# Opening of a hybrid decoder block: first two token tiles transposed before the norm's factor is known, the factor multiplied in later

## The chip, the cores and the metric

The kernel runs on one core of a Trainium2 chip. The core has a matrix engine (TensorE, PE in the profile, with its weight loads as PEld), three engines for elementwise work (VectorE as DVE, ScalarE as ACT, GpSimd as POOL) and SyncE (SP), which here only issues DMA transfers. Every engine works through its own queue in order and waits on semaphores for the others. PE writes to PSUM, eight banks of 128 partitions by 512 fp32 columns; GpSimd works on SBUF alone in this kernel. The metric is device time in microseconds (us).

## What is computed

A decoder block on 512 tokens of width 1024 in fp32: a conformer convolution branch and a gated linear recurrence branch, merged by sigmoid gates, then a SwiGLU mixer and a last norm. The change touches only the first two lines of it:

```python
def rmsnorm(x, g):
    xf = x.astype(jnp.float32)
    y = xf * lax.rsqrt(jnp.mean(xf * xf, axis=-1, keepdims=True) + EPS)
    return (y * g.astype(jnp.float32)).astype(x.dtype)
...
        h = rmsnorm(x, norm1_g[l])
        z = h @ w_in[l] + b_in[l]
        z_glu, z_rx, z_rg, z_ga, z_gb = jnp.split(z, split_idx, axis=-1)
        u = z_glu[..., :D_CONV] * jax.nn.sigmoid(z_glu[..., D_CONV:])
...
        m = jax.nn.sigmoid(z_ga) * y_a + jax.nn.sigmoid(z_gb) * y_b
        x = x + m @ w_mix_out[l]
        h = rmsnorm(x, norm2_g[l])
        x = x + (jax.nn.silu(h @ ffn_w1[l]) * (h @ ffn_w3[l])) @ ffn_w2[l]
    return rmsnorm(x, norm_f_g)
```

The norm's factor belongs to a token: the square root of the mean square of its row of x. The gain g belongs to a channel.

## The kernel before

The 512 tokens are four tiles of 128 (`xt[t][h]`, tile t, half h of the 1024 channels). The products need h with channels on partitions, so x is transposed on PE, 128 by 128 at a time, into PSUM. Eight blocks of channels (c = 0 to 7) make up the 1024. From each transposed block ACT makes a rounded high part and DVE the low part that is left (`h1p[c]`, in the profile h10h, h10l to h17h, h17l); weights are split alike into `hl_in`, high part first. A product is then three matmuls for each block, high by high, low by high, high by low weights (`mm3`, line 525).

The opening (lines 639 to 665) is written out by hand for PE, ACT, DVE and SP: what stands there is the order of these queues. The order of GpSimd and of everything after line 665 is made by a scheduler. PE first runs 21 warm-up matmuls that feed nothing (line 504). `norm1_rows` squares and sums the two halves of a tile on ACT, takes the root there, inverts it on DVE, and DVE multiplies both halves of x by it (line 595). When tiles 0 and 1 are scaled, `turn_half` (line 567) transposes them into banks and splits them (ACT line 582, DVE line 583). These are the first half of the columns, tokens 0 to 255. `early_mm` then multiplies them with the weight chunks in0 and in8, the first two of the order in line 233, into the first half of the banks z0 and z8, and the low products of each come last. Meanwhile tiles 2 and 3 are normed; they are transposed and split, and `early_mm` fills the second halves. z1, the product with chunk in1, is the first on all 512 tokens (`in_mm`, line 675). DVE casts and subtracts in8 itself there, through `Later`; GpSimd subtracts in0.

SP issues the four halves of x0 and x1 first, then a row of gains, then the chunks in0 and in8, 512 KB each, then x2 and x3. Six PSUM banks rotate under the tag "mm", two under "cv"; four raw weight buffers and five split ones rotate too. At most eight transfers are under way, since the ninth waits for the first one's semaphore.

## Time and profile before

| what | us |
|---|---|
| median of 3 runs (lowest, highest) | 797.65 (797.45, 798.82) |
| profiled execution, own time | 797.7 |
| its span, first to last instruction | 795.9 |
| PE busy in the span | 789.2 |
| DVE, ACT, POOL busy | 673.2, 471.7, 228.8 |

The span is what the trace covers; the execution's own time has 1.8 us more around it. In the rows that follow, a timeline row gives start, duration, engine, line of the kernel, operation, what is written from what, shapes and count, and in brackets the idle time of that engine before the row with what ended it. Matmuls overlap, so that the start of one to the start of the next, not the printed duration, is what one costs. A row of a group gives busy time in all and the mean ns of one, then the idle time before them.

### The profile page before, as it was taken

How to read it: one execution, taken by the hardware profiler on the slowest of the kernel's cores; microseconds unless marked ns; L12 is line 12 of the kernel's file. 1: busy time of each engine (PE TensorE's matmuls, PEld its weight loads, DVE VectorE, ACT ScalarE, POOL GpSimd, SP SyncE). 2: the span in 40 equal slices, each digit the busy share in tenths (PEclk: the TensorE clock that was granted, in tenths of full speed). 3: DMA queues.
4: the chain of work that ended last, by engine and by line, in shares of the span. 5: the costliest groups of instructions: out<-in, count | busy, mean ns of one | idle time of the engine just before them, and what ended most of it. 6: DMA issues, size and time to landing. Idle time of an engine off the chain costs nothing.

```text
span 795.9 us, 12177 instructions
## 1 busy us (share of the span) xinstructions
PE 789.2 (99%) x4369; PEld 690.5 (87%) x4369; DVE 673.2 (85%) x1020; ACT 471.7 (59%) x683; POOL 228.8 (29%) x181
## 2 busy tenths in 40 slices
PE   9999999999999999999999999999999999999997
PEld 8888888888888888888888898999999999888885
DVE  6699899999989988786787889978878887889757
ACT  6646585987768855563335575545455555577443
POOL 1855766797666856030000000000000000000000
PEclk9999999999999999999999999999999999999999
DMA  6945646487555664368847545566555553676652
GB/s 213 257 130 143 187 144 208 121 247 208 173 168 173 213 182 120 128 203 263 276 160 243 172 134 158 131 171 181 155 133 133 133 133 106 210 258 207 198 173 106
DMA packets 184604, 140.29 MB, mean 176 GB/s; under 512 B 14259, under 2 KB 162143, under 8 KB 184543
## 3 DMA queue, kind: packets, MB, share of 16 engines
q1 hardware_dynamic: 183103, 134.27, 55.2%
q0 software_dynamic: 1440, 5.24, 3.5%
q8 instruction: 34, 0.56, 0.3%
q14 instruction: 27, 0.22, 0.1%
HBM read 113.79 MB, written 18.64 MB: 166 GB/s over the span
## 4 chain that ended last, share of the span: by engine, by line
PE 99%; DVE 0%; issue 0%; ACT 0%
PE z L534 36%; PE or L953 13%; PE ft L1080 7%; PE yb L534 7%; PE fa L1080 7%; PE fr L1080 6%; PE ya L534 5%; PE mxr L953 5%; PE fe L1080 4%; PE g L827 3%; PE fb L1080 2%; PE f L534 2%; PE warm L506 1%; PE f L1106 1%; PE tx L574 1%; PE th L574 0%
## 5 line engine op out<-in xcount | busy, mean ns | idle before, releaser
L702 DVE SCALAR_TENSOR_TENSOR cv<-u,par,cv 128x511 f32<-128x511 f32 (+19 forms) x240 | 162.4, 730 | 5.0 <-ACT cv L699 4.7
L119 POOL TENSOR_TENSOR hl_in<-raw_in,hl_in 128x1024 fp32r<-128x1024 f32 x51 | 123.5, 2426 | 83.1 <-ACT hl_in L123 69.6
L355 POOL DMA_DIRECT2D raw_fb<-raw_fb x10 | 8.7, 874 | 298.4 <-DVE raw_fb L357 186.1
L119 POOL TENSOR_TENSOR ows<-ows 128x256 f32<-128x256 f32 x66 | 56.7, 861 | 37.7 <-DMA ows<-in_ffn_w_dram 34.7
L123 ACT CAST hl_ft<-raw_fb 128x1024 fp32r<-128x1024 f32 x40 | 41.8, 1048 | 32.5 <-DVE raw_fb L357 17.0
L123 ACT CAST hl_in<-raw_in 128x1024 fp32r<-128x1024 f32 x50 | 52.1, 1043 | 10.4 <-PE z L534 6.6
L119 DVE TENSOR_TENSOR hl_ft<-raw_fb,hl_ft 128x1024 fp32r<-128x1024 f32 x40 | 48.5, 1220 | 7.0 <-ACT hl_ft L123 6.9
L119 DVE TENSOR_TENSOR hl_fb<-raw_fb,hl_fb 128x1024 fp32r<-128x1024 f32 x30 | 36.6, 1221 | 9.5 <-ACT hl_fb L123 9.3
L357 DVE TENSOR_TENSOR raw_fb<-raw_fb,raw_fb 128x1024 f32<-128x1024 f32 x20 | 24.5, 1225 | 20.3 <-DMA raw_fb<-in_ffn_w_dram 20.0
L534 PE MATMUL z<-h10h,hl_in 128*128 128x512 f32 (+1 forms) x108 | 41.5, 385 | 0.0
L534 PE MATMUL z<-h17h,hl_in 128*128 128x512 f32 (+1 forms) x108 | 41.1, 381 | 0.0
L534 PE MATMUL z<-h13h,hl_in 128*128 128x512 f32 (+1 forms) x108 | 41.1, 381 | 0.0
L534 PE MATMUL z<-h15h,hl_in 128*128 128x512 f32 (+1 forms) x108 | 41.1, 381 | 0.0
L534 PE MATMUL z<-h14h,hl_in 128*128 128x512 f32 (+1 forms) x108 | 41.1, 381 | 0.0
L534 PE MATMUL z<-h16h,hl_in 128*128 128x512 f32 (+1 forms) x108 | 41.1, 381 | 0.0
L534 PE MATMUL z<-h12h,hl_in 128*128 128x512 f32 (+1 forms) x108 | 41.1, 381 | 0.0
L534 PE MATMUL z<-h11h,hl_in 128*128 128x512 f32 (+1 forms) x108 | 41.1, 381 | 0.0
L123 ACT CAST hl_fb<-raw_fb 128x1024 fp32r<-128x1024 f32 x30 | 31.4, 1047 | 8.9 <-PE mxr L953 3.7
L119 DVE TENSOR_TENSOR hl_ob<-raw_ob,hl_ob 128x1024 fp32r<-128x1024 f32 (+1 forms) x23 | 27.0, 1174 | 11.0 <-ACT hl_ob L123 10.9
L123 ACT CAST hl_ob<-raw_ob 128x1024 fp32r<-128x1024 f32 (+1 forms) x23 | 23.3, 1015 | 21.6 <-PE or L953 10.8
L1080 PE MATMUL fe<-hs_0h,hl_ft 128*128 128x256 f32 x160 | 30.7, 283 | 0.0
L1080 PE MATMUL ft<-hs_1h,hl_ft 128*128 128x256 f32 x160 | 30.4, 283 | 0.0
(1016 smaller groups left out, 2610.0 us busy)
## 6 DMA issues: line engine op xcount, KB each, us to landing
raw_in<-in_w_in_dram SPq DMA_DIRECT2D x52, 512.0 KB
raw_fb<-in_ffn_w_dram SPq DMA_DIRECT2D x96, 256.0 KB
ows<-in_ffn_w_dram SPq DMA_DIRECT2D x44, 256.0 KB
os<-ows SPq DMA_DIRECT2D x22, 512.0 KB
raw_ob<-in_ffn_w_dram SPq DMA_DIRECT2D x33, 256.0 KB
raw_ot<-os SPq DMA_DIRECT2D x33, 256.0 KB
raw_lo<-in_lru_w_out_dram SPq DMA_DIRECT2D x16, 320.0 KB
raw_fb<-raw_fb POOLq DMA_DIRECT2D x10, 512.0 KB, 4.6
```

The source lines that it names most:

```text
L119: return eng.tensor_tensor(out=o, in0=x, in1=y, op=ALU.subtract)
L123: copy(h, full)
L355: pool_e.dma_start(out=q, in_=y, accum_op=ALU.add)
L357: vec.tensor_tensor(out=q, in0=q, in1=y, op=ALU.add)
L506: pe.matmul(wp[:, :P], ones, ones, start=True, stop=True)
L534: pe.matmul(ps, l, r, start=i == 0, stop=i == n - 1)
L574: pe.transpose(ps[:, t * P : (t + 1) * P], src, ident)
L702: vec.scalar_tensor_tensor(out=acc[c][:, s:], in0=u[c][:, : T - s], scalar=dw(c, s), in1=acc[c][:, s:], op0=ALU.mult, op1=ALU.add)
L827: pe.matmul(ps, l, r, start=k == 0, stop=k == len(mms) - 1)
L953: pe.matmul(banks[i], l_[:, ts], r_, start=start and n == 0, stop=stop and n == 2, skip_group_check=again)
L1080: pe.matmul(ps[:, HALVES[i]], lw[:, 4 * i + c, :], rx_, start=not (again or i or c or m), stop=bool(i and c == 3 and m == 2), skip_group_c ...
L1106: pe.matmul(plain_1[:, cs], l, r, start=k == 0 and m == 0, stop=k == ND - 1 and m == 2)
```

## The change

The first two tiles are transposed as they land, half a tile at a time, and unscaled: `load_x` issues single halves, in0's chunk is loaded and cast in two halves (`FirstChunk`), and the first half of z0's product starts when the first four blocks of channels of x0 and x1 are there. Two `plain` sets of split tiles hold the unscaled blocks. The warm-up is 6 matmuls ahead and 1 between. The norm's factor of a token is laid on the diagonal of a 128 by 128 tile (`dg`) and multiplied by ones, which puts it on all partitions with tokens along columns (`rp`, copied to `rbc`). It multiplies the first halves of z0 and z8 in place (`scale_early`), and the kept transposes of tiles 0 and 1, whose scaled blocks (`scaled`) are split into the first halves of `h1p` for z1 and all later products. GpSimd is now in the order written by hand, casts in8 and in1 besides, and makes four of the eight low parts of tiles 0 and 1.

```diff
-WARM = 21
+WARM = 6, 1
...
+    PAIRED = (0, 4, 1, 5, 2, 6, 3, 7)
...
+    def place(banks, c):
+        return banks[c % 4][:, HALVES[c // 4]]
+    def turn_rows(banks, t, cs):
+        for c in cs:
+            pe.transpose(place(banks, c)[:, (t % 2) * P : (t % 2 + 1) * P], xt[t][c // 4][:, (c % 4) * P : (c % 4 + 1) * P], ident)
+    def split_rows(banks, hf, cs):
+        for c in cs:
+            ps = place(banks, c)
+            g = pc("norm1_g", c)
+            h, l = parts_in(hf)[c]
+            act.activation(h, ps, AF.Copy, scale=g)
+            vec.scalar_tensor_tensor(out=l, in0=ps, scalar=g, in1=h.bitcast(F32), op0=ALU.mult, op1=ALU.subtract)
...
+        def cast(self, h):
+            cs = slice(h * T, (h + 1) * T)
+            vec.tensor_copy(self.hl[:, 0, cs], self.raw[:, cs])
+            sub(pool_e, self.hl[:, 1, cs], self.raw[:, cs], self.hl[:, 0, cs].bitcast(F32))
...
-    with tc.manual_schedule(engines={ET.PE, ET.Activation, ET.DVE, ET.SP}):
-        norm1_rows(0)
-        norm1_rows(1)
+    with tc.manual_schedule(engines={ET.PE, ET.Activation, ET.DVE, ET.SP, ET.Pool}):
+        w0 = FirstChunk()
+        load_x(0, [0])
+        load_rows(first[0])
+        load_x(1, [0])
+        w0.load(0)
+        load_x(0, [1])
+        load_x(1, [1])
+        w0.load(1)
+        warm_up(WARM[0])
         rows_turned(0, ROWS[0][1])
...
+        turn_rows(banks0, 0, range(4))
+        turn_rows(banks0, 1, range(4))
+        warm_up(WARM[1])
+        w0.cast(0)
+        split_rows(banks0, 0, range(4))
...
+        early_mm(0, 0, range(4), (0, 1))
+        turn_rows(banks0, 0, range(4, 8))
+        turn_rows(banks0, 1, range(4, 8))
+        early_mm(0, 0, range(4), (2,))
...
+        split_rows(banks0, 0, range(4, 6))
+        dg = shortt("dg")
+        for t in range(2):
+            vec.tensor_scalar(out=dg[:, t * P : (t + 1) * P], in0=ident, scalar1=r[t], scalar2=None, op0=ALU.mult)
+        split_rows(banks0, 0, range(6, 8))
+        early_mm(0, 0, range(4, 8), (0, 1))
...
+        emit_to(2, pool_e.tensor_copy)
+        early_mm(0, 0, range(4, 8), (2,))
+        rp = bank2("rp")
+        for t in range(2):
+            pe.matmul(rp[:, t * P : (t + 1) * P], ones, dg[:, t * P : (t + 1) * P], start=True, stop=True)
...
+        def scale_early(i):
+            ps = early[i][2][:, HALVES[0]]
+            vec.tensor_tensor(out=ps, in0=ps, in1=rbc, op=ALU.mult)
+        def scaled(c):
+            f = scaled1[c // 2][:, HALVES[c % 2]]
+            vec.scalar_tensor_tensor(out=f, in0=place(banks0, c), scalar=pc("norm1_g", c), in1=rbc, op0=ALU.mult, op1=ALU.mult)
...
+        for c in (2, 6, 3, 7):
+            scaled(c)
+        for c in (2, 6, 3, 7):
+            scaled_parts(c, vec)
...
-        mm3(ps, ws, h1)
+        mm3(ps, [ws[k] for k in PAIRED], [h1[k] for k in PAIRED])
```

Three places of the queues. First ACT, from its first square of x (n1j00 is tile 0, half 0; tx00 to tx07 are the banks of the transposes) on; before:

```order
L550 ACTIVATE n1j00_185,stats_162<-x00_114 128x512
L556 ACTIVATE n1j01_186,stats_162<-x01_115 128x512
L557 ACTIVATE stats_162<-stats_162 128x1
L550 ACTIVATE n1j10_194,stats_162<-x10_116 128x512
L556 ACTIVATE n1j11_195,stats_162<-x11_117 128x512
L557 ACTIVATE stats_162<-stats_162 128x1
L582 ACTIVATE h10h_163<-tx00_211,par_108 128x256
L582 ACTIVATE h11h_165<-tx01_216,par_108 128x256
```

and with the change (hp0h to hp3h hold the high parts of the unscaled blocks, two blocks each; tx00 to tx03 are banks of two blocks):

```order
L559 ACTIVATE n1j00_193,stats_136<-x00_114 128x512
L627 ACTIVATE hp0h_153<-tx00_189,par_108 128x256
L627 ACTIVATE hp0h_153<-tx01_190,par_108 128x256
L627 ACTIVATE hp1h_155<-tx02_191,par_108 128x256
L627 ACTIVATE hp1h_155<-tx03_192,par_108 128x256
L565 ACTIVATE n1j01_194,stats_136<-x01_115 128x512
L566 ACTIVATE stats_136<-stats_136 128x1
L559 ACTIVATE n1j10_195,stats_136<-x10_116 128x512
L565 ACTIVATE n1j11_196,stats_136<-x11_117 128x512
L566 ACTIVATE stats_136<-stats_136 128x1
L627 ACTIVATE hp2h_157<-tx00_189,par_108 128x256
L627 ACTIVATE hp2h_157<-tx01_190,par_108 128x256
```

Four copies moved ahead of three of the squares; the other four stay behind them.

Second SP, its first transfers; before:

```order
L490 DMA x00_114<-in_x_dram 128x512
L490 DMA x01_115<-in_x_dram 128x512
L490 DMA x10_116<-in_x_dram 128x512
L490 DMA x11_117<-in_x_dram 128x512
L483 DMA rows0_109<-in_norm1_g_dram 8x128
L167 DMA raw_in0_206<-in_w_in_dram 128x8x128
L167 DMA raw_in8_251<-in_w_in_dram 128x8x128
L490 DMA x20_118<-in_x_dram 128x512
```

and with the change:

```order
L500 DMA x00_114<-in_x_dram 128x512
L493 DMA rows0_109<-in_norm1_g_dram 8x128
L500 DMA x10_116<-in_x_dram 128x512
L660 DMA raw_in0_171<-in_w_in_dram 128x4x128
L500 DMA x01_115<-in_x_dram 128x512
L500 DMA x11_117<-in_x_dram 128x512
L660 DMA raw_in0_171<-in_w_in_dram 128x4x128
L150 DMA raw_in8_268<-in_w_in_dram 128x8x128
L500 DMA x20_118<-in_x_dram 128x512
```

The first half of x1 moved up from third to second of the large transfers, half of the weights to third; the second halves of x0 and x1 moved down.

Third POOL, from its first subtraction of weights; before, these were

```order
L119 TENSOR_TENSOR hl_in0_208<-raw_in0_206,hl_in0_208 128x1024
L119 TENSOR_TENSOR hl_in1_384<-raw_in1_382,hl_in1_384 128x1024
L119 TENSOR_TENSOR hl_in9_439<-raw_in9_437,hl_in9_439 128x1024
L119 TENSOR_TENSOR hl_in16_478<-raw_in16_476,hl_in16_478 128x1024
L119 TENSOR_TENSOR hl_in17_483<-raw_in17_481,hl_in17_483 128x1024
```

and with the change (hq0 and hq2 hold scaled blocks):

```order
L119 TENSOR_TENSOR hl_in0_172<-raw_in0_171,hl_in0_172 128x512 x2
L123 CAST hl_in8_292<-raw_in8_268 128x1024
L119 TENSOR_TENSOR hl_in8_292<-raw_in8_268,hl_in8_292 128x1024
L119 TENSOR_TENSOR h10l_138<-hq0_161,h10h_137 128x256
L119 TENSOR_TENSOR h14l_146<-hq2_163,h14h_145 128x256
L123 CAST hl_in1_377<-raw_in1_274 128x1024
L119 TENSOR_TENSOR hl_in1_377<-raw_in1_274,hl_in1_377 128x1024
L119 TENSOR_TENSOR h11l_140<-hq0_161,h11h_139 128x256
L119 TENSOR_TENSOR h15l_148<-hq2_163,h15h_147 128x256
L119 TENSOR_TENSOR hl_in9_424<-raw_in9_280,hl_in9_424 128x1024
```

Two casts, one whole subtraction (in8) and four quarter ones are new there.

More of the change, by code (lines that the diff above doesn't have):

```diff
@@ L161, in emit_chunk @@
         rv = raw[:, :n]
-        if where == "made":
+        if where in ("made", "there"):
             pass
@@ L504, in tile_block, with warm_up @@
     wp = bank2("warm")
-    for _ in range(WARM):
-        pe.matmul(wp[:, :P], ones, ones, start=True, stop=True)
+    def warm_up(n):
+        for _ in range(n):
+            pe.matmul(wp[:, :P], ones, ones, start=True, stop=True)
     first = [i for i, (lo, _, _) in enumerate(parts) if lo < n_first]
-    load_x(0)
-    load_x(1)
-    load_rows(first[0])
     def rows_turned(c0, c1):
@@ new lines, in tile_block, with early_mm, row_junk @@
+    todo_in = {}
+    def early_mm(i, hf, ks, parts):
+        _, ws, ps = early[i]
+        for k in ks:
+            (wh, wl), (xh, xl) = ws[k], parts_in(hf)[k]
+            for n in parts:
+                l, r = ((wh, xh), (wh, xl), (wl, xh))[n]
+                left = todo_in.setdefault((i, hf), 3 * ND)
+                todo_in[i, hf] = left - 1
+                pe.matmul(ps[:, HALVES[hf]], l, r, start=left == 3 * ND, stop=left == 1)
+    def row_junk(t):
+        return [shortt(f"n1j{t}{h}") for h in range(2)]
@@ new lines, in tile_block @@
+        scaled(4)
+        scaled_parts(0)
+        scaled_parts(4)
+        scaled(1)
+        scaled(5)
+        scale_early(0)
+        scale_early(1)
+        banks1 = [b(f"tx1{i}") for i, b in enumerate((bank2, bank2, bank, bank))]
+        turn_rows(banks1, 2, PAIRED)
+        turn_rows(banks1, 3, PAIRED)
+        emit_to(3, pool_e.tensor_copy)
+        split_rows(banks1, 1, range(8))
+        scaled_parts(1)
+        scaled_parts(5)
+        for k in range(4):
+            for i in range(2):
+                early_mm(i, 1, [k], (0, 1))
```

98 lines of the change are left out of this document (69 added, 29 removed).

## The prediction

> **What bounds the kernel now.** I read the page's busy times first, then the chain of waits in order of time.
>
> ```profile
> span 795.9 us, 12177 instructions
> PE 789.2 (99%) x4369; PEld 690.5 (87%) x4369; DVE 673.2 (85%) x1020; ACT 471.7 (59%) x683; POOL 228.8 (29%) x181
> ```
>
> ```profile
> 1.09 7.80 PE warm L506 x42
> 8.89 0.15 PE par_ps L517
> 9.04 1.90 PE tx L574 x16
> 10.94 6.51 PE z L534 x48
> 17.45 2.13 PE tx L574 x16
> 19.58 2.87 PE z L534 x24
> 22.44 0.07 PE par_ps L517
> 22.52 2.92 PE z L534 x24
> 25.43 0.29 PE par_ps L517 x3
> 25.72 43.59 PE z L534 x192
> ...
> 685.94 104.37 PE or L953 x458
> ```
>
> The reader is to see that TensorE (PE) never rests between 1.09 and 790 us, so that the time is the sum of its matmuls plus a start of 1.1 and a tail of 5.6 us. The only part of that sum that makes nothing is the 7.80 us of warm-up. It stands for the time until both tiles of the first half are loaded, normed and scaled. All the change can do is to begin the real work earlier than 8.89, and it must hand that lead on to the first full-width product, z1, which begins at 25.72 in the chain.
>
> The next view splits the warm-up at 7.08 (start:end, length, PE busy and passes).
>
> ```profile
> 1.08:7.08 6.00, 5.99 (x28) 1.00 0.82 258
> 7.08:8.83 1.75, 1.75 (x16) 1.00 1.18 315
> ```
>
> 28 passes in 6.00 us are 0.214 each, 16 in 1.75 are 0.109: the matrix clock doubles at about 7.1 us, though the column of the granted clock (1.00) does not show it. Work brought forward into the first 7 us thus runs at half speed.
>
> **The change part by part.** *Removed and added on PE.* 21 warm-up matmuls of two passes become 7: 28 passes fewer, of which 16 at 0.109 and 12 at 0.214 are 4.3 us. Added are the two matmuls that spread the norm's factor over all partitions (rp): 4 passes, 0.45 us. The 32 transposes and 96 half-width products stay. At most 3.9 us can be won, and only if what feeds PE keeps up. So I follow the feeders.
>
> ```profile
> 3.41 0.63 ACT L550 ACTIVATE n1j<-x 128x512 f32<-128x512 f32 x1 [0.99 <-DMA x<-in_x_dram]
> 4.41 0.63 ACT L556 ACTIVATE n1j<-x 128x512 f32<-128x512 f32 x1 [0.27 <-DMA x<-in_x_dram]
> 5.81 0.63 ACT L550 ACTIVATE n1j<-x 128x512 f32<-128x512 f32 x1 [0.36 <-DMA x<-in_x_dram]
> 6.54 0.63 ACT L556 ACTIVATE n1j<-x 128x512 f32<-128x512 f32 x1
> 7.30 0.30 ACT L557 ACTIVATE stats<-stats 128x1 f32<-128x1 f32 x1
> 9.45 0.47 ACT L582 ACTIVATE h10h<-tx,par 128x256 fp32r<-128x256 f32 x1 [1.85 <-PE tx L574]
> 9.82 0.47 ACT L582 ACTIVATE h11h<-tx,par 128x256 fp32r<-128x256 f32 x1
> 9.16 0.68 DVE L123 CAST hl_in<-raw_in 128x1024 fp32r<-128x1024 f32 x1
> 9.96 0.48 DVE L583 SCALAR_TENSOR_TENSOR h10l<-tx,par,h10h 128x256 fp32r<-128x256 f32 x1
> 10.36 0.48 DVE L583 SCALAR_TENSOR_TENSOR h11l<-tx,par,h11h 128x256 fp32r<-128x256 f32 x1
> ```
>
> *Landings.* ScalarE (ACT) waited for the first, second and third transfer of 256 KB until 3.41, 4.41 and 5.81; the fourth kept nobody past 6.54. The SyncE queue now brings x0 first half, x1 first half, first half of in0's weights, x0 and x1 second halves, second half of the weights, all 256 KB. I give these slots 3.4, 4.4, 5.8, 6.6, 7.4 and 8.4 (the last two one slot of about 0.9 further each).
>
> *First half of z0.* 12 warm passes of 0.214 end at 3.7; the transpose of the gains and four of x0 at half speed take PE to 4.8, four of x1 to 5.6, the single warm-up matmul to 6.0. ACT's first copy of a transposed bank can start some 0.4 after its last transpose (9.45 against the second transpose in the old order), so at 5.3, then every 0.36 (9.82 - 9.45): free at 6.75. VectorE (DVE) casts half of the weights (half of 0.68) once they are there, 5.8 to 6.15, and then makes four low parts, one every 0.39 (10.36 - 9.96), to 7.7. PE's eight products run between 6.1 and 7.9. The first product starts 4.6 us earlier than the old 10.7. That lead does not last.
>
> *Second half of z0.* PE does eight transposes and four low products, to about 9.4. But ACT, free at 6.75, has three squares and two roots ahead of the next copies: a square takes 0.73 (6.54 - 5.81), a root 0.2 to 0.3, so 3 x 0.73 + 0.5 puts the fifth copy at 9.4, its end at 9.9. DVE's low parts follow at 0.39 with two multiplications for the diagonal between them. Such a multiplication is priced from the first row below, a quarter of 0.483, so 0.13 with rounding up: the eighth low part is ready at 9.9 + 3 x 0.39 + 0.26 + 0.48 = 11.8. PE, which stands still for some 1.5 us in here, ends z0's half at 12.0, four low products at 12.5, rp at 13.0.
>
> ```profile
> L595 DVE TENSOR_SCALAR x<-x,stats 128x512 f32<-128x512 f32 x8 | 3.5, 483 | 0.1
> L558 DVE RECIPROCAL stats<-stats 128x1 f32<-128x1 f32 x4 | 0.6, 162 | 2.5 <-ACT stats L557 2.5
> L119 POOL TENSOR_TENSOR hl_in<-raw_in,hl_in 128x1024 fp32r<-128x1024 f32 x10 | 23.9, 2401 | 25.8 <-ACT hl_in L123 14.3 <-DVE hl_in L123 8.6 <-issue 2.9
> L119 POOL TENSOR_TENSOR hl_gate<-raw_gate,hl_gate 128x512 fp32r<-128x512 f32 x1 | 1.3, 1284 | 2.0 <-ACT hl_gate L123 2.0
> L215 POOL MEMSET raw_gate<- 128x512 f32 x2 | 1.1, 528 | 0.1
> ```
>
> *in8's weights go to GpSimd (POOL).* Its cast of 1024 columns is not in this trace. Below it lies the fill (0.53 for 512 columns, so 1.06), above it the two-input subtraction, 2.40. DVE casts the second half of in0's weights at 8.6 (behind its statistics), so POOL ends their subtraction (1.28) at 10.2, so the cast is done at 11.3 to 12.6, before PE wants it at 13.0, and the low part at 13.7 to 15.0, wanted at 13.0 + 16 x 0.12 = 14.9. I take the middle, 1.7: hidden, with 1.1 us to spare for the high and 0.6 for the low part; beyond that it costs PE one for one. [...]
>
> *From z8 on.* The marks are z8's first product, the transposes, the second half, z1.
>
> ```profile
> 14.40 0.28 PE L534 MATMUL z<-h10h,hl_in 128*128 128x256 f32 x1
> ...
> 17.28 2.30 PE L574 MATMUL tx<-ident,x 128*128 128x128 f32 x16
> 19.33 0.36 PE L534 MATMUL z<-h10h,hl_in 128*128 128x256 f32 x1
> ...
> 25.52 0.47 PE L534 MATMUL z<-h10h,hl_in 128*128 128x512 f32 x1
> ```
>
> Before, z8's first product to z1's took 25.52 - 14.40 = 11.12 us. The changed PE queue holds the same instructions in that stretch (24 products, 16 transposes, 48 products, four transposes of parameters). New are waits for DVE, which now has between 11.8 and the second half: four small statistics steps (0.16, so 0.2 with the step between), three scalings of x2 and x3 (0.45), the copy of rp, four scaled transposes and the two half banks (0.39 each): 0.8 + 1.35 + 7 x 0.39 = 4.9, and about 0.6 waiting for ACT's root at 12.5. It is done at 17.3. The last pair of banks that the transposes need comes free at 16.5, where PE asks at 16.6; the first new low part is ready at 18.3 or so, where PE's transposes are over at 17.9. I take 0.3 for both, bounded by 0 and 0.8. z1 then starts at 13.0 + 11.1 + 0.3 = 24.4, **1.1 us earlier**.
>
> *After z1* the products are the same in the same order (only the order of the eight inner blocks differs), so 1.1 us reaches the end. Its new inputs have cover: DVE's last four scaled blocks and low parts end near 24.0 and are wanted at 24.4 + 12 x 0.23 = 27.1; POOL's two low parts behind in1's cast end before 22.7, wanted at 25.8. If that cover were gone, each us would be a us. DVE's convolution steps start later by the added work, into this hole:
>
> ```profile
> 32.57 3.90 DVE L702 SCALAR_TENSOR_TENSOR cv<-u,par,cv 128x511 f32<-128x511 f32 x5 [3.86 <-ACT cv L699]
> ```
>
> The profiled execution took 797.7 us (span 795.9), the runs' median is 797.65. 797.7 - 1.1 = **796.6 us**, span 794.8. The unknown ends (landings 0.5 later, cast, waits 0 to 0.8, roots) give 796.0 to 797.4 for this case.
>
> **The rivals.** *The gain is larger because the old opening suffers more from the clock.* The old opening is a number of passes: every us by which the doubling comes later than 7.1 costs 1 - 0.109/0.214 = 0.49 us. The new one waits for ACT between 9.4 and 12.0, so a doubling up to about 10 us costs it nothing. With the doubling 1 to 3 us later in the runs it is compared with, the gain is 1.6 to 2.6, about 795.7. For it: the three runs before scatter from 797.45 to 798.82, as a moving doubling would make them; against it: the profiled execution lies at the median. [...]
>
> *Slower: PE stays at half speed.* The old opening keeps PE busy without a gap for 6 us before the doubling. The new one has gaps, at 4.8 to 5.6 if x1 is late, at 7 to 8 behind DVE and from 9.4 to 12.0 behind ACT. If these hold the doubling back past 12.5, rp and z8's first half pay 0.105 per pass or product: 28 x 0.105 = 2.9 us, and the 64 instructions of the second half up to 6.7 more. It decides from a doubling later than about 15 us; at 18 it makes 797.7 - 1.1 + 2.9 = 799.5. Against it: at half speed PE itself is the slower side until about 10 us, so the gaps close while it is cold. [...]
>
> *Nothing is left.* POOL's cast takes over 3 us, or the half transfers land a us later than taken, and z8 starts at 14.4 as before: 797.7, give or take 0.5. For it: all feeders are within a us of deciding, and SyncE issues more and smaller transfers early; against it: even a cast of 2.40 fits.
>
> **How the numbers follow.** Forecast 0.52, larger gain 0.26, slower 0.12, nothing 0.10. 0.2% is 1.6 us, about what a measurement of this kernel tells from no change, so the bounds are 796.05 and 799.25. Faster: 0.12 of the forecast's 0.52 and 0.23 of the larger gain, 0.35. Slower: 0.11 of the cold case. Within: the rest, 0.54. The range leaves out the ends of the larger gain and of the cold case: 795.3 to 798.9.
>
> **What would show it.** Right: warm-up of 12 passes, first product near 6.1, PE idle some 1.5 us between 9 and 12, released by ACT and DVE; z8 at 13.0, z1 at 24.4, no PE idle after it; POOL's cast between 1.1 and 2.4. Wrong: products of 0.21 after 10 us (cold); PE released by POOL at z8 (cast); ACT's fifth copy away from 9.4; z1 later than 25.5; any PE wait past 30 us.

## The result, and the profile after

The changed kernel is slower: 801.75 us (median of 6 runs, 801.2 to 804.6) against 797.69 (6 runs, 797.13 to 798.82), a ratio of 1.0057 with a 95% interval of 1.004 to 1.0075. The forecast was 796.6, the range up to 798.9. The profiled execution of the changed kernel, 804.6, is the slowest of its six runs, so its rows show more loss than a typical run has.

| mark in the profile, us | before | predicted | after |
|---|---|---|---|
| first product of z0 | 10.70 | 6.1 | 7.75 |
| fifth copy of a transposed bank on ACT | – | 9.4 | 10.99 |
| z8's first product | 14.40 | 13.0 | 17.74 |
| z1's first product | 25.52 | 24.4 | 29.43 |
| span | 795.9 | 794.8 | 802.8 |

The page's busy times after the change:

```profile
span 802.8 us, 12165 instructions
PE 789.4 (98%) x4345; PEld 689.6 (86%) x4345; DVE 680.9 (85%) x1031; ACT 474.5 (59%) x691; POOL 236.4 (29%) x189
```

PE has 24 matmuls fewer than before and is as long busy (789.4 against 789.2). Part of what was removed ran at half speed (0.214 us a pass up to 7.08, 0.109 after), and now other work does (granted clock 0.50 from 8.18 to 11.59 and from 15.01 to 18.42). The other 6.7 us of span are rest. The chain of waits up to z1 tells where (start, length, what):

```profile
2.00 5.15 DMA raw_in<-in_w_in_dram
7.16 0.02 issue
7.18 0.44 DVE hl_in L666
7.62 0.14 issue
7.75 2.13 PE z L640 x8
9.88 1.08 PE tx L620 x5
...
10.99 0.48 ACT hp2h L627
...
12.37 2.55 DVE dg L732 x2
14.92 0.41 DVE hp3l L628
...
27.59 2.19 DVE h12l L119
29.77 2.54 DVE h16l L119
32.32 2.54 DVE h13l L119
34.86 0.04 issue
34.90 2.14 PE z L543 x8
```

Before, this chain was PE alone from 1.09 on. Now it begins with the transfer of in0's first half, which lands at 7.16, and then runs through VectorE twice: 2.55 us for the two small multiplications of `dg`, and 2.2 to 2.5 us for each low part of 256 columns. PE's own waits in the whole span:

```profile
PE z L640 <- DVE hp3l L628: 2.4, 1, 2.4
PE z L640 <- DVE hl_in L666: 1.7, 1, 1.7
PE warm L518 <- DVE ones L509: 1.1, 1, 1.1
PE z L543 <- DVE h13l L119: 0.9, 1, 0.9
PE g L970 <- DMA ext6h<-xb7h: 0.8, 1, 0.8
PE fe L1223 <- DVE hl_ft L119: 0.2, 1, 0.2
```

Only the 1.1 behind `ones` was there before. The timeline of VectorE and GpSimd, at `dg` and again behind the second half, shows what runs beside these small operations while they last so long:

```profile
11.36 1.04 POOL L123 CAST hl_in<-raw_in 128x1024 fp32r<-128x1024 f32 x1
12.29 2.63 DVE L732 TENSOR_SCALAR dg<-ident,stats 128x128 f32<-128x128 f32 x2
12.48 2.35 POOL L119 TENSOR_TENSOR hl_in<-raw_in,hl_in 128x1024 fp32r<-128x1024 f32 x1
...
27.09 7.47 POOL L119 TENSOR_TENSOR hl_in<-raw_in,hl_in 128x1024 fp32r<-128x1024 f32 x3
27.50 2.27 DVE L119 TENSOR_TENSOR h12l<-hq,h12h 128x256 fp32r<-128x256 f32 x1
29.70 2.62 DVE L119 TENSOR_TENSOR h16l<-hq,h16h 128x256 fp32r<-128x256 f32 x1
32.24 2.60 DVE L119 TENSOR_TENSOR h13l<-hq,h13h 128x256 fp32r<-128x256 f32 x1
34.77 0.41 DVE L119 TENSOR_TENSOR h17l<-hq,h17h 128x256 fp32r<-128x256 f32 x1
```

Each long VectorE row ends with a GpSimd row: `dg` at 12.29 + 2.63 = 14.92, the subtraction at 14.83. The next three low parts end some 2.5 us apart, once for each GpSimd subtraction, and the fourth, when GpSimd is idle (27.09 + 7.47 = 34.56), takes 0.41. The row of the tile `dg` alone (shortest, median, longest in ns) separates its two halves: one took 0.275 us, the other was held for 2.441.

```profile
L732 DVE TENSOR_SCALAR dg<-ident,stats x2: 275/1358/2441, 12.3 to 12.5; 128x128 f32<-128x128 f32 x2
```

Last, the clock. Four windows (start:end, length, busy time of PE, PEld, DVE, ACT and POOL with counts, granted clock, DMA share, GB/s):

```profile
4.77:8.18 3.41, 1.62 (x11) 1.07 (x10) 1.00 (x3) 1.86 (x5) 0.49 (x1) 1.00 0.97 306
8.18:11.59 3.41, 3.41 (x16) 3.41 (x17) 1.81 (x8) 2.85 (x10) 2.23 (x3) 0.50 1.10 352
11.59:15.01 3.42, 1.34 (x10) 1.03 (x8) 3.42 (x5) 2.18 (x7) 3.17 (x2) 1.00 1.07 303
15.01:18.42 3.41, 3.05 (x14) 3.05 (x15) 2.16 (x8) 1.21 (x4) 0.00 (x0) 0.50 0.37 95
```

After each of the two windows in which PE was busy for less than half (1.62 of 3.41 and 1.34 of 3.42), the next ran at 0.50: PE rests until 7.75 for its weights and pays from 8.18 to 11.59, and rests for `dg` and pays from 15.01 to 18.42.

### The profile page after: what moved, and what is told of

Its sections match the earlier page's. It is cut to its first block, busy times and chain, and to the rows that moved or that the text cites. A ratio compares the mean times of both kernels' runs of the same rounds, so it can differ in the third digit from the quotient of the medians.

```text
span 802.8 us, 12165 instructions
## 1 busy us (share of the span) xinstructions
PE 789.4 (98%) x4345; PEld 689.6 (86%) x4345; DVE 680.9 (85%) x1031; ACT 474.5 (59%) x691; POOL 236.4 (29%) x189
## 4 chain that ended last, share of the span: by engine, by line
PE 87%; DVE 6%; POOL 3%; DMA 2%; issue 1%; ACT 0%; SPq 0%; POOLq 0%; DVEq 0%
PE z L543 27%; PE or L1096 13%; PE ft L1223 7%; PE yb L543 7%; PE fa L1223 6%; PE ya L543 5%; PE mxr L1096 5%; PE fr L1223 4%; PE fe L1223 3%; PE g L970 2%; PE fb L1223 2%; POOL hl_in L119 2%; PE f L543 1%; DMA raw_in<-in_w_in_dram 1%; PE z L640 1%
## 5 line engine op out<-in xcount | busy, mean ns | idle before, releaser
L845 DVE SCALAR_TENSOR_TENSOR cv<-u,par,cv 128x511 f32<-128x511 f32 (+18 forms) x240 | 162.1, 728 | 1.9 <-ACT cv L842 1.7
L119 POOL TENSOR_TENSOR hl_in<-raw_in,hl_in 128x1024 fp32r<-128x1024 f32 (+1 forms) x53 | 126.3, 2389 | 77.6 <-ACT hl_in L123 65.4
L543 PE MATMUL z<-h10h,hl_in 128*128 128x512 f32 x100 | 39.1, 391 | 0.0
L543 PE MATMUL z<-h14h,hl_in 128*128 128x512 f32 x100 | 38.9, 389 | 0.0
L543 PE MATMUL z<-h17h,hl_in 128*128 128x512 f32 x100 | 38.9, 389 | 0.0
L543 PE MATMUL z<-h13h,hl_in 128*128 128x512 f32 x100 | 38.9, 389 | 0.0
L543 PE MATMUL z<-h11h,hl_in 128*128 128x512 f32 x100 | 38.9, 389 | 0.0
L543 PE MATMUL z<-h15h,hl_in 128*128 128x512 f32 x100 | 38.9, 389 | 0.0
L543 PE MATMUL z<-h12h,hl_in 128*128 128x512 f32 x100 | 38.9, 389 | 0.0
L543 PE MATMUL z<-h16h,hl_in 128*128 128x512 f32 x100 | 38.9, 389 | 0.0
```

The costliest lines, as they stand in the source:

```text
L119: return eng.tensor_tensor(out=o, in0=x, in1=y, op=ALU.subtract)
L543: pe.matmul(ps, l, r, start=i == 0, stop=i == n - 1)
L845: vec.scalar_tensor_tensor(out=acc[c][:, s:], in0=u[c][:, : T - s], scalar=dw(c, s), in1=acc[c][:, s:], op0=ALU.mult, op1=ALU.add)
```

## The experiments

Three theories stood against each other. The hold: VectorE waits for GpSimd where it works inside SBUF while GpSimd runs, at `dg` (2.63 us) and at three of the last four low parts (2.27 to 2.62). The clock: PE's rest before its first product lets the clock fall (0.50 from 8.18), and all later work is late for that. The landings: the halves of x and of the weights come too late for any order of the opening. The times below are device us, with the ratio to the kernel before in the same series and its 95% interval. "Marks" are first product, fifth copy, z8, z1 in that kernel's profile.

**First series: one suspect each, and all three.**

`dg_act` makes `dg` on ScalarE:

```diff
-            vec.tensor_scalar(out=dg[:, t * P : (t + 1) * P], in0=ident, scalar1=r[t], scalar2=None, op0=ALU.mult)
+            act.activation(dg[:, t * P : (t + 1) * P], ident, AF.Copy, scale=r[t])
```

> The two multiplications that make dg go from VectorE to ScalarE, nothing else. Theory (VectorE's two small multiplications, 2.63 us for both, were held up by GpSimd's subtraction of in8's weights that ran from 12.48 to 14.83): VectorE makes hp3's low parts right behind hp2's, near 12.3 to 13.1; PE's wait of 2.4 us for hp3l falls under 0.4; z1 starts between 25.8 and 27.0 instead of 29.4. The last four low parts are still held up behind z1's start and give some of it back, so the median is 798.0 to 800.5. Rival (everything was late because the weights and ScalarE's copies were late): the wait for hp3l stays over 1.5 us, z1 starts after 28.5, the median is 801 to 802.

Measured 802.13 (801.71 to 802.54, 4 runs), 1.005 [1.0035, 1.0065]; marks 7.90, 11.17, 14.98, 26.56. PE's wait for hp3l is gone and z1 is 2.9 us earlier than in the changed kernel's profile, as the theory had it. The median, expected at 798.0 to 800.5, gains nothing: the two profiles are of runs of 801.74 and 804.6. None of the four runs is above 802.54, where the changed kernel had 803.65 and 804.6, but four runs do not show that the long ones are gone.

`low_psum` keeps the last four scaled blocks in their PSUM banks, so that the low parts read one operand from PSUM:

```diff
-            scaled(c)
+            scaled(c, place(banks0, c))
...
-            scaled_parts(c, vec)
+            scaled_parts(c, vec, place(banks0, c))
```

> The last four scaled blocks of the first half (2, 6, 3, 7) are written back into the PSUM bank they come from, so that VectorE's subtraction for the low part reads one input from PSUM and one from SBUF instead of two from SBUF. Theory (a VectorE operation with both inputs in SBUF waits for GpSimd's subtraction to end): the four low parts take 0.4 to 0.5 us each instead of 2.3 to 2.6, all end before 30 us, PE waits for none of them; z1 still starts near 29.4; the median is 0.9 to 1.5 below 801.75, so 800.2 to 800.9. Rival (VectorE is only late, and the length of the rows is the queue's): the rows stay over 2 us and the median at 801 to 802.

Measured 803.13 (800.23 to 804.11, 5 runs), 1.0059 [1.0039, 1.0078]; marks 7.59, 10.40, 15.41, 27.53. The time misses (800.2 to 800.9 was expected), the mechanism holds, as VectorE's and GpSimd's timeline shows:

```profile
26.22 0.42 DVE L119 TENSOR_TENSOR h12l<-tx,h12h 128x256 fp32r<-128x256 f32 x1 [0.25 <-ACT h12h L123]
28.40 0.42 DVE L119 TENSOR_TENSOR h16l<-tx,h16h 128x256 fp32r<-128x256 f32 x1 [1.76 <-ACT h16h L123]
28.74 0.41 DVE L119 TENSOR_TENSOR h13l<-tx,h13h 128x256 fp32r<-128x256 f32 x1
31.48 0.42 DVE L119 TENSOR_TENSOR h17l<-tx,h17h 128x256 fp32r<-128x256 f32 x1 [2.33 <-ACT h17h L123]
...
25.19 9.50 POOL L119 TENSOR_TENSOR hl_in<-raw_in,hl_in 128x1024 fp32r<-128x1024 f32 x4
```

0.41 to 0.42 us each in the middle of GpSimd's four subtractions: with one of the two operands in PSUM, none of these four operations was held. The time won is given back, since two of ScalarE's high parts now stand behind other casts (1.76 and 2.33 us of idle time before two low parts), and the clock fell in this run too, to 0.50 from 13.64 on.

`warm9` sets `WARM = 6, 9`: eight more warm-ups between the transposes and the first product.

> Nine warm-up matmuls instead of one in the gap between the first half's transposes and its products. Theory (the clock fell back because PE rested from 6.1 to 7.75 us, but what sets z8's start is VectorE): the granted clock stays at 1.0 from its first rise until past 12 us, the products before 12 us take 0.12 instead of 0.21, and PE only waits longer for hp3l; z8 starts within 0.4 us of 17.74 and the median is 801.0 to 802.0. Rival (the clock itself cost the time): z8 starts over 1.5 us earlier and the median is below 800.3.

Measured 801.27 (800.91 to 801.93, 4 runs), 1.004 [1.0025, 1.0055]; marks 8.04, 10.63, 14.83, 26.39. The time is the theory's, but z8 is 2.9 us earlier, as the rival had it. The clock no longer falls (the passes of rp last 0.27 us each, where the changed kernel has 0.42), and `dg`, two multiplications as before, takes

```profile
11.91 1.01 DVE L732 TENSOR_SCALAR dg<-ident,stats 128x128 f32<-128x128 f32 x2
...
11.60 1.04 POOL L123 CAST hl_in<-raw_in 128x1024 fp32r<-128x1024 f32 x1
12.72 2.43 POOL L119 TENSOR_TENSOR hl_in<-raw_in,hl_in 128x1024 fp32r<-128x1024 f32 x1
```

1.01 where it took 2.63: it now comes early enough to meet the cast (over at 12.64) instead of the subtraction. So the length of the hold went with the GpSimd operation that `dg` met, 1.04 us for the cast and 2.35 for the subtraction of the changed kernel. In the five profiles with `dg` on VectorE it took 2.63 and 2.58 where the clock had fallen before it (the changed kernel, twice) and 1.01 where it had not (`low_psum`, `warm9`, `low_pool9`). That this separates the long runs of the changed kernel from its usual ones fits these rows, but is not shown: both of its profiles are of long runs.

`three` makes all three edits.

> The three edits together: dg on ScalarE, the last four low parts from PSUM, nine warm-up matmuls. Theory: no row of VectorE under GpSimd's subtractions is longer than 0.5 us before 30 us, the clock stays at 1.0 from its first rise on, z8 starts between 14.0 and 15.0 (ScalarE's fifth copy near 11.0, its eighth near 12.1, the last low part near 12.9, then 1.3 us of products and rp), z1 between 25.3 and 26.3, and the median is 797.0 to 798.5, the level of the kernel before. Rival (what is lost lies in later waits, in16's weights or the copies of the gates): z1 starts as early, but the median stays over 799.5.

Measured 799.67 (798.75 to 800.33, 10 runs), 1.002 [1.001, 1.0029]; marks 8.20, 10.81, 14.60, 26.55. Expected was 797.0 to 798.5; a loss remains.

**Second series: the hold by itself, and what remains.**

`probe` is the kernel before with six VectorE operations added in a place where GpSimd subtracts weights:

```diff
+        vec.memset(px, 1.0)
+        vec.scalar_tensor_tensor(out=py[:, :256], in0=pp[:, :256], scalar=1.0, in1=px[:, :256], op0=ALU.mult, op1=ALU.mult)
+        vec.tensor_tensor(out=pp[:, 256:512], in0=px[:, :256], in1=py[:, :256], op=ALU.subtract)
+        vec.tensor_scalar(out=pp[:, :256], in0=px[:, :256], scalar1=2.0, scalar2=None, op0=ALU.mult)
+        vec.tensor_copy(pz[:, :256], px[:, 256:])
+        vec.tensor_scalar(out=pw[:, :P], in0=ident, scalar1=2.0, scalar2=None, op0=ALU.mult)
```

> The kernel before with six spare operations of VectorE put at about 28.7 us, where it has nothing to do and GpSimd subtracts weights without a pause from 27.4 to 34.5 us; their results are used by nothing. In order: a fill of 512 columns in SBUF; a scaled product with one input from PSUM and one from SBUF, 256 columns, to SBUF; a subtraction of two SBUF inputs, 256 columns, to PSUM; a multiplication by a number from SBUF to PSUM, 256 columns; a copy from SBUF to SBUF, 256 columns; the multiplication by a number from SBUF to SBUF, 128 columns (dg's). [...]

Measured 797.47 (one run; before in this series 797.63). The timeline of both engines:

```profile
28.45 0.48 DVE L667 MEMSET probe<- 128x512 f32 x1
28.97 0.42 DVE L668 SCALAR_TENSOR_TENSOR probe<-par_ps,probe 128x256 f32<-128x256 f32 x1
29.43 2.40 DVE L669 TENSOR_TENSOR par_ps<-probe,probe 128x256 f32<-128x256 f32 x1
31.86 0.43 DVE L670 TENSOR_SCALAR par_ps<-probe 128x256 f32<-128x256 f32 x1
...
21.93 9.61 POOL L119 TENSOR_TENSOR hl_in<-raw_in,hl_in 128x1024 fp32r<-128x1024 f32 x4 [9.57 <-ACT hl_in L123]
33.13 2.40 POOL L119 TENSOR_TENSOR hl_in<-raw_in,hl_in 128x1024 fp32r<-128x1024 f32 x1 [1.59 <-ACT hl_in L123]
```

Beside the same GpSimd work a fill takes 0.48, an operation with one PSUM operand 0.42, one with two SBUF operands 2.40, from 29.43 to 31.83, with the fourth subtraction over at 31.54. The last three operations fell into GpSimd's pause from 31.54 to 33.13 and test nothing; so for the kind of operation that `dg` is, the hold is read from its own rows alone.

`low_pool3` is `dg_act` and `warm9` with the last four low parts on GpSimd (`scaled_parts(c, vec)` becomes `scaled_parts(c)`), one behind another there and none on VectorE.

> dg on ScalarE and nine warm-up matmuls as in the run of three edits, but the last four low parts go to GpSimd, ahead of its three weight subtractions, and stay in SBUF, so that ScalarE's order of casts is that of the changed kernel. Theory: the four low parts take 0.75 us each on GpSimd and end before 29 us; PE waits for none of them, nor for the gates' copies near 180 us; z1 near 26.4 and nothing lost behind it, so the median is 798.6 to 799.2 (z1's 0.9 us over the kernel before, 797.9). Rival (GpSimd's weight subtractions, now 3 us later, are what is waited for): PE waits 0.5 us or more for hl_in behind 30 us, median over 799.8.

Measured 799.0 (798.4 to 800.52, 11 runs), 1.0018 [1.0009, 1.0027]; marks 8.05, 10.65, 14.44, 26.39. On GpSimd the four low parts take 0.73 to 0.74 each. PE no longer waits for any of them, and 1.4 us are still lost. Its profile is of its slowest run, 800.52.

`copies_first` is `low_pool3` with all eight copies of transposes ahead of the second tile's squares and root, rp behind z8's first products, and the first tile's second half turned between z0's first products.

```diff
-        early_mm(0, 0, range(4), (0, 1))
+        early_mm(0, 0, range(2), (0, 1))
         turn_rows(banks0, 0, range(4, 8))
+        early_mm(0, 0, range(2, 4), (0, 1))
...
+        split_rows(banks0, 0, range(4, 8))
+        begun.append(rstd_begin(xt[1][0], jk[1][0]))
```

> As the run before it in this list (low parts on GpSimd), and in the opening ScalarE makes its fifth to eighth copies ahead of the squares of the second tile, PE turns the first tile's second half between the products, and the matmuls that spread the factor stand behind z8's products instead of ahead of them. Theory (after the rests are gone, z8's start is set by ScalarE's copies, which stand behind the squares, and by rp): the fifth copy starts near 10.0 instead of 10.8, z8 at 13.0 to 13.6 instead of 14.6, z1 0.5 to 1.2 us earlier than in the run before it, the median 797.4 to 798.6. Rival (z8's start is set by the landing of in0's weights and GpSimd's cast of in8's, near 12.9): z8 is not below 13.8 and the time falls by less than 0.4.

Measured 800.49 (799.56 to 801.36, 5 runs), 1.0036 [1.0023, 1.005]; marks 8.32, 10.10, 13.01, 27.08. The fifth copy and z8 are where the theory had them (10.0, and 13.0 to 13.6), although the clock rose only at 6.91 in this profile (four or five passes of PE in each half us up to 6.5, seven from 7.5 on) and the nine warm-ups held the first product back to 8.3. But the factor is ready and spread later: `dg` is finished at 13.85, where `low_pool3` has it at 12.05, and PE's transposes of tiles 2 and 3 wait until the scaled blocks have been made from the banks that they need:

```profile
18.47 0.44 PE L620 MATMUL tx<-ident,x 128*128 128x128 f32 x2 [1.07 <-DVE hq L764]
```

From z8 to z1 it takes 14.07 us instead of 11.95 in `low_pool3`, and the lead of 1.4 us at z8 is gone at z1.

`wide` is `three` with in0's halves read as rows of 2 KB from other columns, so z0's first chunk is not the reference's:

```diff
+            nc.sync.dma_start(self.raw[:, h * T : (h + 1) * T], a["w_in"][0][h * P : (h + 1) * P, :T])
```

> The run of three edits, but in0's weights come as two transfers of 128 rows of 2 KB instead of 512 pieces of 512 bytes (they are other numbers of the same matrix, so z0 is left out of what is computed). Theory (VectorE's cast of in0's first half stood at 7.2 to 7.6 instead of the 5.8 that was predicted because pieces of 512 bytes come at 220 GB/s instead of 310 to 340): the cast starts between 6.0 and 6.8, the second half of x0 is squared before 7.6, z8 starts 0.6 to 1.2 us earlier than the 14.6 of that run. Rival (three transfers of 256 KB at once just take so long, whatever their pieces): the cast starts after 7.2 and z8 within 0.3 of 14.6.

Measured 799.78 (one run), in0's first half landed at 7.52 (7.60 in `three`). In this one run larger pieces do not bring it sooner.

**Third series: the changed kernel again, and other orders of landing.**

`after2` is the changed kernel, unedited.

> The changed kernel once more, for a second profile of it. Theory (its time has a plain part and an accident: when the clock falls back at about 8 us, the two multiplications for dg come late enough to meet GpSimd's subtraction of 2.4 us instead of its cast of 1.0 us; without the accident dg costs about 1 us): a run near 801.5 shows z1 between 26.3 and 27.5, dg at about 1.0 us, the last four low parts held up as before and PE waiting about 1 us for h13l; a run near 804 shows dg at 2.6 us and z1 near 29.4. Rival (dg's length is not what makes the slow runs): a run below 802 with dg over 2 us, or one above 803 with dg near 1.

Measured 806.93 (one run); marks 8.34, 11.61, 18.30, 31.18. `dg` took 2.58 with one half held for 2.384. A window with PE busy for 1.25 of 3.42 us (4.66 to 8.08) went ahead of one at a granted clock of 0.50, and a second one, 1.93 of 3.41 (11.49 to 14.90), too. Neither 801.5 nor 804 came, but `dg` is long in a long run again, so the bad case of the first profile is no single event. By the other runs of the changed kernel it is not the usual one.

`x_first` is `low_pool3` with the four halves of x ahead of the weights (x0, gains, x1, x0, x1, then in0 twice):

> The run with low parts on GpSimd (799.0), with both tiles of x loaded whole before in0's weights, as in the kernel before; nothing else is moved. Theory (z8's start is set by ScalarE's fifth copy, and that by the landing of x0's second half near 8.1, because in0's first half of weights is ahead of it in the queue): x0's second half is squared from 6.7 to 7.0 on, the fifth copy starts near 9.6 instead of 10.7, in0's first half is cast near 7.4 as before, z8 starts between 13.2 and 13.9 instead of 14.4, the median is 0.4 to 1.1 below that run's, 797.9 to 798.6. Rival (all transfers up to 9 us land late whatever the order): the fifth copy is not before 10.4 and the median within 0.3 of 799.0.

Measured 800.33 (799.22 to 800.9, 5 runs), 1.0034 [1.0021, 1.0046]; marks 9.11, 11.55, 15.36, 27.04. In the order of the change, a half of weights or of x lands last at 3.54, 5.17, 7.16, 7.86, 8.57, 9.45; in this order at 3.49, 5.01, 6.54, 7.48, 8.51, 9.45. The slots stay, the third but for 0.6 us, and their owners change.

`x_first_turn` goes on from there: all transposes and all eight copies ahead of z0's first product, four warm-ups between, rp behind z8's first products.

> As the run before it in this list, and PE turns the second halves before z0's first product, ScalarE makes all eight copies before it squares the other three halves, VectorE makes the first four low parts before it casts weights, the factor's matmuls stand behind z8's first products, and there are four warm-up matmuls between the two turnings. Theory: the fifth copy starts near 7.4, z0's half is done near 11, z8 starts between 11.5 and 12.8, PE then waits 0.3 to 1.5 us for the second half of the tokens, z1 is between 24.6 and 25.6 and the median 796.8 to 798.0: at best 1 us below the kernel before. Rival (in8's weights and x2, x3 land no sooner, so the opening has nothing to give): z1 is later than 25.9 and the median over 798.3.

Measured 801.74 (799.81 to 803.07, 5 runs), 1.0047 [1.0034, 1.0061]; marks 9.90, 9.64, 14.55, 28.22. The fifth copy is early, though not at the 7.4 expected, the clock rose only at 10.33 (18 passes in the 3.42 us before), and z8 comes as late as in `low_pool3`. Behind it PE waits 0.93 and 0.34 us for scaled blocks, as in `copies_first`.

**Fourth series: is it the transfers?**

`rows_later` is `low_pool3` with the gains' transfer behind x1's first half (`load_rows(first[0])` one line lower).

> The run with low parts on GpSimd (799.0), with the small transfer of the gains behind x1's first half in SyncE's queue instead of ahead of it. Theory (a transfer of any size takes SyncE about 0.4 us to issue, and all behind it land that much later): x1's first half lands 0.3 to 0.5 earlier, near 4.5; nothing else moves by more than 0.1, since in0's weights and x0's second half stay where they were in the queue; the fifth copy stays near 10.7 and the median within 0.4 of 799.0. Rival (x1's landing holds the chain up to z8): z8 starts 0.3 us or more earlier than 14.44 and the median falls by 0.3 to 0.6.

Measured 799.77 (798.52 to 802.31, 11 runs), 1.0023 [1.0014, 1.0032]; marks 8.49, 10.27, 14.08, 25.80. The best z8 of the versions that spread the factor ahead of it, yet no better time.

`two_queues` is `low_pool3` with both halves of x1 and the gains issued by ScalarE, `WARM = 6, 4`.

> The run with low parts on GpSimd, with x1's two halves and the gains issued from ScalarE's queue at the start and x0 and in0's weights from SyncE's, and four middle warm-up matmuls instead of nine. Theory (the first landings are late because SyncE issues one transfer each 0.4 to 0.5 us and the DMA engines are not full before 6 us): in0's first half is cast between 5.2 and 6.4, x0's second half squared from 6.8 to 7.3, the fifth copy near 9.6, z8 between 13.0 and 13.7, z1 between 25.0 and 25.8, the median 797.3 to 798.4. Rival (the DMA engines are the limit): the cast is not before 7.0, z8 not before 14.1, the median over 798.6.

Measured 801.66 (799.89 to 801.96, 5 runs), 1.0043 [1.003, 1.0056]; marks 7.55, 11.0, 15.44, 27.71. The second half of x0 landed at 8.46, where `low_pool3` has 8.11. With four warm-ups the clock fell here as well, to 0.50 from 14.02 to 17.43, so this run does not separate the two queues from the clock.

`before_two` is the kernel before with x1's halves issued by ScalarE and 17 warm-ups:

```diff
-WARM = 21
+WARM = 17
...
-    load_x(1)
+    load_x(1, act)
```

> The kernel before, with x1's two halves issued from ScalarE's queue and 17 warm-up matmuls instead of 21; the change is not in it. Theory (two queues bring x1 0.5 to 1 us earlier): x1 is scaled by 7.9 instead of 8.7, the first transposes start near 8.2 and the first product near 10.0 instead of 10.7, and the median is 0.4 to 0.9 below the kernel before. Rival (the DMA engines are the limit, or in0's weights hold the first product at 10.7 all the same): within 0.3 of the kernel before.

Measured 799.23 (798.61 to 799.86, 11 runs), 1.0016 [1.0007, 1.0025]; first product 11.49, z1 26.47. The first scaling of x began at 7.77 instead of 5.69. Issuing from two engines made the old opening slower, with no fall of the clock (1.00 up to 12.61): the halves of x0 are squared from 4.51 and 6.49 on instead of 3.41 and 4.41. Why they come later is not shown.

**Fifth series.** `low_pool9` is `low_pool3` with `dg` back on VectorE: the change with two edits alone, nine warm-ups and no low part on VectorE.

> The run with low parts on GpSimd and nine warm-up matmuls, with dg on VectorE again as in the changed kernel. Theory (with the clock up, dg meets only GpSimd's cast, and VectorE then waits about as long as ScalarE's copies are put off by making dg: 0.6 us): dg lasts 0.9 to 1.1 us, the last low part stands within 0.3 us of the 12.44 it has with dg on ScalarE, z1 within 0.4 of 26.36, the median between 798.5 and 799.8, no run over 802. Rival (dg on VectorE costs by itself what it lasts): z1 0.8 us or more later and the median over 800.0, with runs over 802 where dg meets the subtraction.

Measured 799.38 (11 runs: ten from 798.23 to 799.71 and one of 803.25), 1.0021 [1.001, 1.0033]; marks 7.55, 10.14, 14.33, 25.91. `dg` takes 1.01 again. The run of 803.25 (none over 802 was expected) has no profile and stays unexplained. Against `low_pool3` the place of `dg` is worth nothing that these runs can tell. No version beats the kernel before.

## Why the prediction was wrong, point by point

**The step that failed** is the price of small VectorE operations. "Second half of z0" had the two multiplications for the diagonal at 0.13 each, and "After z1" had the last four low parts at some 0.4 each, done near 24.0 and wanted at 27.1. Both prices came from rows in which GpSimd rested. Measured: the pair of multiplications takes 2.63, 2.58 or 1.01, according to the GpSimd operation that it meets, and a low part 2.27 to 2.62 where its operands are in SBUF, 0.42 where one is in PSUM, 0.41 when GpSimd is idle. In the profile of the changed kernel h17l is done at 35.2, 11 us later than the forecast had it; 5 of these are z1's own lateness (29.43 for 24.4), and the other 6 are more than the cover of 3.1 us. The rows of before held the warning, and I did not read them: two of its tiny operations on 10 columns, beside a subtraction of weights on GpSimd,

```profile
23.12 1.11 DVE L623 TENSOR_SCALAR bh<-par 128x10 f32<-128x10 f32 x2
...
21.74 2.39 POOL L119 TENSOR_TENSOR hl_in<-raw_in,hl_in 128x1024 fp32r<-128x1024 f32 x1 [9.41 <-ACT hl_in L123]
```

ended at 24.23, with it (24.13), while the operations around them took 0.17. With two SBUF operands an operation took 2.40 beside GpSimd's subtractions, with one in PSUM 0.42 (`probe`); what it is in the two engines that makes VectorE wait, no run shows.

**What it is worth.** By medians, `warm9` (no fall of the clock, short hold of `dg`) is 0.5 under the changed kernel, `low_pool9` (low parts off VectorE as well) 1.9 under `warm9` and 1.6 over the kernel before in its own series (the series have kernels before of 797.63 to 797.94). The first step is within the scatter of the runs. The second changes only which engine makes four low parts: all four runs of `warm9` lie above ten of the eleven of `low_pool9`, and PE's wait of 1.0 for h13l goes. The intervals of the changed kernel and of `low_pool9` do not overlap (1.004 to 1.0075 against 1.001 to 1.0033). So the hold and the clock together are shown as a cause, by the two ratios (1.0057 and 1.0021) of more than half of the loss; the split between them is an estimate from medians.

**"Landings"** were 0.8 to 1.4 us too early from the second slot on: x1's first half 5.17 for 4.4, in0's first half 7.16 for 5.8, the second halves of x 7.86 and 8.57 for 6.6 and 7.4. The weights' half landed between 7.0 and 7.7 in all other profiles with this order but `copies_first` (5.74). That moves the first product from 6.1 to 7.75, and **the fifth copy** from 9.4 to 10.99: ScalarE's timeline shows its two waits,

```profile
7.89 0.63 ACT L565 ACTIVATE n1j<-x 128x512 f32<-128x512 f32 x1 [0.73 <-DMA x<-in_x_dram]
...
10.99 0.84 ACT L627 ACTIVATE hp2h<-tx,par 128x256 fp32r<-128x256 f32 x2 [0.50 <-PE tx L620]
```

0.73 for x0's second half and 0.50 for PE's transposes, which ran at a clock of 0.50 (from 8.18 to 11.59). By these rows it is the likeliest reason why the lead of 1.1 us at z1 does not come back with the hold gone; no run brought all the halves in sooner. The order that brings x sooner brings weights later (`x_first`), and two queues and larger pieces did not help. In `rows_later` the first half of in0 landed at 6.51 and x0's second half at 7.52, sooner than in `low_pool3` (7.45 and 8.11), and the median is no better. With nothing held long and the factor spread ahead of z8, z8 starts at 14.1 to 14.4 (`rows_later`, `low_pool9`, `low_pool3`), as in the kernel before, and z1 0.3 to 0.9 later. That is the rival "Nothing is left", with half transfers a us later than taken. `copies_first` marks its limit: there in0's first half landed at 5.74 and z8 started at 13.01, both as forecast, but with the factor put behind the copies, so the lead was lost before z1.

**"After z1 ... 1.1 us reaches the end"** failed too, and it took the tail behind the last matmul as unchanged. The profile of `low_pool9`, of its median run, has a span 1.7 over the kernel before's (797.6 for 795.9). Of this 0.4 is there at z1 (25.91 for 25.52) and 1.2 at the last matmul (791.15 for 789.91). Most of what is added between them comes behind the transfer `ext6h`, whose matmul starts at 181.69 instead of 180.73; why it lands later is not settled. The last 0.45 arises behind the last VectorE operation, in the kernel before and in `low_pool9`:

```profile
791.58 0.75 DVE L1221 SCALAR_TENSOR_TENSOR of<-or,stats,gfh 128x512 f32<-128x512 f32 x1
```

```profile
792.82 0.75 DVE L1364 SCALAR_TENSOR_TENSOR of<-or,stats,gfh 128x512 f32<-128x512 f32 x1
```

From there it is 3.57 us to the end of the span before and 4.03 now. The traces of the two kernels show SyncE going through the semaphores of the transfers in the same order, about 0.06 us each where one has landed. Before, that of the last output transfer is in the last of ten such waits (it lands at 795.01); in the changed kernel it is in the third, and the seven others follow its landing (801.49), the last at 801.93. From the end of the last VectorE operation to the end of the span it is 3.98 to 4.04 us in the profiles of the changed kernel, `dg_act`, `low_psum`, `warm9`, `three` and `low_pool9`. The change issues one transfer more, in0's second half, which fits a shift by one place; no run tested it.

**"Slower: PE stays at half speed"** had the side right, the size (799.5) too small, and the mechanism in part. It asked for a doubling that comes too late. In fact the clock rose early (full by 4.77) and fell to 0.50 again after PE had rested (busy for 1.62 us of the 3.41 from 4.77 on). In the two profiles of bad runs (804.6 and 806.9) the fall brings late copies, `dg` in front of the subtraction, a wait behind it (2.4 us in the first) and another fall. That a typical run (801.2 to 801.8) goes without this is inferred from `warm9`.

**Right:** the first copy of a transposed bank (5.59 for 5.3), GpSimd's cast at the lower end (1.04 for 1.06 to 2.40, 1.7 taken), the stretch from z8 to z1 (11.69 for 11.4, though 0.7 us of it ran at a clock of 0.50), PE's sum as the bound where it does not wait. The change saved the passes that it was said to save, and could not feed PE in the time won.

## What to carry to other kernels

Price a small VectorE operation whose operands are all in SBUF by the GpSimd operation that runs beside it, not by its own size (here `dg` took 1.01 beside a cast and 2.63 beside a subtraction): look in the trace for short operations that end with a GpSimd row, and try such work with a PSUM operand (0.42 in `low_psum`), or on GpSimd itself (0.73 to 0.74 in `low_pool3`). Before work is moved forward into an opening, list which transfer each new first step waits for by its last part, since a warm-up that looks empty may stand for nothing but those landings. When PE has less to do in the opening, look at the clock of the window after each rest (0.50 here after windows with 1.25 to 2.34 us of work in 3.41). And follow the first early mark to the first step that needs everything: z8 came at 13.01 once, and z1 was late all the same.

## What the hardware showed that was not expected

*The hold cost GpSimd something as well.* Three GpSimd subtractions took 7.47 us in the changed kernel, with a VectorE operation let in between each two of them, and 7.13 without (`low_pool9`). By an estimate from these two, each of the two exchanges cost GpSimd some 0.17, while VectorE's three operations there took 2.27 to 2.62 instead of 0.41.

*Some windows that were only partly idle were followed by half the clock.* Where the granted clock fell and rose again it did so in steps of 3.41 us. Counted in these steps from where the clock rose, these windows at full clock were followed as shown (PE busy in the window):

| kernel, window | PE busy, us | clock in the next |
|---|---|---|
| dg_act, 4.77:8.18 | 1.25 | 0.50 |
| after, 4.77:8.18 and 11.59:15.01 | 1.62, 1.34 | 0.50 |
| after2, 11.49:14.90 | 1.93 | 0.50 |
| copies_first, 17.15:20.56 | 2.00 | 1.00 |
| before_two, 5.79:9.20 | 2.07 | 1.00 |
| two_queues, 10.61:14.02 | 2.23 | 0.50 |
| low_psum, 10.23:13.64 | 2.34 | 0.50 |
| low_pool9, 11.78:15.19 | 2.59 | 1.00 |

The windows of `low_psum` and `low_pool9`, with the one after each:

```profile
10.23:13.64 3.41, 2.34 (x13) 1.54 (x12) 2.82 (x8) 3.02 (x9) 3.33 (x3) 1.00 1.09 351
13.64:17.05 3.41, 3.41 (x17) 3.41 (x17) 2.75 (x7) 1.93 (x6) 1.30 (x1) 0.50 0.81 206
```

```profile
11.78:15.19 3.41, 2.59 (x20) 2.29 (x20) 2.95 (x8) 2.74 (x9) 2.81 (x2) 1.00 1.10 302
15.19:18.60 3.41, 3.41 (x30) 3.20 (x30) 3.34 (x11) 1.77 (x6) 1.14 (x2) 1.00 0.34 84
```

In `low_psum` PE had work for 2.34 us of 3.41, and the next window ran at 0.50. No single bound on busy time fits all rows, since 2.00 was enough in `copies_first` and 2.07 in `before_two`. What is counted stays open.

*The last parts of one transfer set its landing.* The 16 parts of in0's first half landed in the changed kernel at

```
4.87 4.94 5.06 5.13 5.15 5.28 5.29 5.30 5.32 5.43 5.47 5.55 5.92 6.47 6.79 7.16
```

Twelve are there by 5.55, close to the forecast's 5.8, and the last comes 1.6 us later. Why the last four lag was not tried.
